# Low probabilities of two key tiles in the array's column halves, and a paced order of the attention's TensorE work

## The chip, the cores and the metric

The kernel runs on one core of one Trainium2 chip. The metric is the device time of one execution in microseconds. TensorE (PE) multiplies and transposes, ScalarE (ACT) and VectorE (DVE) work on tiles, GpSimd (POOL) and SyncE (SP) mostly issue DMAs here. Each engine takes its instructions in a fixed order.

## The reference

A decoder trunk of two layers, for one sequence of 2048 tokens and a model width of 1024, in float32: a Mamba-2 layer, then multi-head latent attention with 16 heads, a SiLU gate and an output projection, then a last RMS norm. The change is in the attention alone:

```python
def causal_block_attention(q_nope, q_rope, k_nope, k_rope, v):
    ...
        s = jnp.einsum('bqhd,bkhd->bhqk', q_nope[:, q0:kv_len], k_nope[:, :kv_len]) + \
            jnp.einsum('bqhr,bkr->bhqk', q_rope[:, q0:kv_len], k_rope[:, :kv_len])
        s = s.astype(jnp.float32) * scale
        mask = (q0 + local)[:, None] >= jnp.arange(kv_len)[None, :]
        p = jax.nn.softmax(jnp.where(mask, s, -jnp.inf), axis=-1).astype(v.dtype)
        outs.append(jnp.einsum('bhqk,bkhd->bqhd', p, v[:, :kv_len]))
```

A head has 96 score channels (64 + 32) and 64 value channels.

## The kernel before

The program runs the Mamba-2 layer, the projections of the second layer, then the attention (`heads`), then the output projection (`back`). Operands are kept as pairs: a value rounded to a shorter format (high) and what the rounding left (low), so that a few fast products give nearly float32.

**Jobs and rows.** The attention goes by jobs: one head and one block of 512 queries (`qb`, 0 to 3), 64 jobs in all. A job has four rows of 128 queries. A row's keys, up to the diagonal, are cut into score tiles of 256 to 512 keys: one tile a row in block 0, up to four in block 3. A score tile is three matmuls (high by high, high by low, low by high; lines L85, L86, L87 in `mm3`) into one PSUM bank tagged `mm`, of which there are four, and on a row's last tile a product that adds the mask (L903 or L905). VectorE takes each tile's maximum (L906) and, when the row is complete, the negated maximum of those (`nm`, L910). ScalarE then writes the exponentials of each tile (`Pr`, L918) with their sum. A bank is free for the score tile four later when its exponential is done. The exponentials of a row are emitted one by one ahead of the next tiles' score matmuls (`late`).

**Units.** A unit is one job and 128 keys (`kb`). `turn` transposes its probabilities with four TensorE transposes (fewer on the diagonal; L933) into a PSUM bank tagged `tr`, and `pair16` takes the bank to two float16 tiles: the high part on ScalarE (L116, "high copy"), the rest on VectorE (L117, "low copy", which reads the high one). `values` multiplies both with the values: the stationary operand `vals[h][:, kb, :]` holds 64 columns of high values and 64 of low values, so one matmul gives both halves of the output bank `O` (also `tr`, four banks in all). L943 is the product with the high probabilities, L944 the one with the low. `finish` takes the bank to memory (`Os`, L950), where a second DMA adds the lower 64 rows to the upper 64.

**What sets the order.** Inside the attention TensorE runs in the order in which the program is written (a manual schedule for this engine). ScalarE and VectorE are put in order by the scheduler of the tile framework. In TensorE's order, `ahead` emits the score tiles, and after each tile, from the 21st on (`LAG`), a table `CREDIT` says for this block, row and tile which work follows: T a turn, V the pair of value products of a unit turned at least two units ago (`DEPTH`). The work of a row stands mostly after its last tile.

Of the kernel before, what the change touches and what calls it, by code (L numbers as in the profile page):

```python
# [20 lines left out]
P = 128  # L21
# [17 lines left out]
EV0 = ['big', 'Xp', 'big', 'Sp', 'wsp']  # L39
EV1 = ['big', 'yT', 'Xp', 'big', 'Sp']  # L40
LAG = 20
DEPTH = 2
CREDIT = (
    (("VT",), ("TV",), ("VT",), ("TV",)),
    (("", "VTVT"), ("", "TTVV"), ("", "TTVV"), ("", "TTVV")),
    (("TT", "", "VVTV"), ("TV", "", "VTTV"), ("TV", "", "TTVV"), ("TTV", "", "TVV")),
    (("T", "", "", "VVTTVTV"), ("T", "V", "", "VTTVTV"), ("T", "V", "V", "TVTTV"), ("TV", "V", "", "TVTVT")),
)
MAGIC = 12582912.0
PSCALE = 32768.0  # L50
TINY = 2.0 ** -100
# [17 lines left out]
class Net:  # L69
# [793 lines left out]
    def heads(self, sp):  # L863
# [15 lines left out]
        def scores(h, qb, st):  # L879
# [8 lines left out]
            for j in range(4):  # L888
                qs = slice(j * P, (j + 1) * P)
                parts = cuts(qb * TB + (j + 1) * P)  # L890
                nb = len(parts)
                mx = self.t(sp, "mx", [P, 4], bufs=4)
                banks = []
                for n, (c0, w) in enumerate(parts):
                    if late:
                        late.pop(0)()
                    begun.append(0)
                    s = self.t(self.pp, "tr" if len(begun) <= 18 and len(begun) % 2 == 1 else "mm", [P, TB], bufs=4)
                    ks = slice(c0, c0 + w)
# [6 lines left out]
                    v.tensor_reduce(mx[:, n:n + 1], s[:, :w], AX.X, ALU.max)  # L906
                    banks.append((s, w))
                    yield CREDIT[qb][j][n]
                nm = self.t(sp, "nm", [P, 1], bufs=4)
                v.tensor_reduce(nm, mx[:, :nb], AX.X, ALU.max, negate=True)  # L910
                p = {}
                sm = self.t(sp, "sm", [P, 4], bufs=4)
                st["P"].append(p)

                def exp(n, j=j, nb=nb, parts=parts, banks=banks, nm=nm, p=p, sm=sm):
                    s, w = banks[n]
                    x = self.t(sp, "Pr", [P, TB], bufs=NP)
                    nc.scalar.activation(x[:, :w], s[:, :w], AF.Exp, bias=nm, accum_out=sm[:, n:n + 1])  # L918
# [9 lines left out]
        def turn(h, qb, kb, st):  # L928
# [3 lines left out]
            for j in range(jj, 4):  # L932
                nc.tensor.transpose(pt[:, j * P:(j + 1) * P], st["P"][j][kb], self.ident)  # L933
            c = slice(jj * P, TB)
            u = self.t(sp, "PTs", [P, 2, TB], F16, bufs=5)
            self.pair16(u[:, 0, c], u[:, 1, c], pt[:, c], PSCALE)
            return u[:, :, c], c

        def values(h, qb, kb, st, u, c):
            if kb == 0:  # L940
                st["O"] = self.t(self.pp, "tr", [P, TB], bufs=4)
            nk = 4 * qb + 4
            nc.tensor.matmul(st["O"][:, c], vals[h][:, kb, :], u[:, 0], start=kb == 0, stop=False)  # L943
            nc.tensor.matmul(st["O"][:, c], vals[h][:, kb, :], u[:, 1], start=False, stop=kb == nk - 1)  # L944
            if kb == nk - 1:
                finish(h, qb, st)

        def finish(h, qb, st):
# [19 lines left out]
        states = [{"P": []} for _ in jobs]  # L968
        sums = {}
        def ahead():  # L970
            for n, (h, qb) in enumerate(jobs):
                if qb == 0:
                    sums[h] = self.t(sp, "sum", [P, 16], bufs=3)
                yield from scores(h, qb, states[n])

        units = [(h, qb, kb, states[n]) for n, (h, qb) in enumerate(jobs) for kb in range(4 * qb + 4)]
        held = []

        def work(what):

            if what == "T" and units:
                a = units.pop(0)
                held.append((a, turn(*a)))
            elif what == "V" and held and (len(held) > DEPTH or not units):
                a, (u, c) = held.pop(0)
                values(*a, u, c)

        step = 0
        for credit in ahead():
            step += 1  # L990
            if step > LAG:
                for what in credit:
                    work(what)
        while units or held:
            work("T")
            work("V")


    def back(self):
# [190 lines left out]
```

## Time and profile before

| | us |
|---|---|
| median of three runs | 3243.08 |
| lowest, highest | 3242.1, 3247.14 |
| profiled execution | 3238.15 |
| its span | 3236.3 |
| attention, first score tile to last value product | about 2128 to 3050 of the span |
| TensorE busy | 3156.2 (98%) |
| VectorE busy | 2593.4 (80%) |
| ScalarE busy | 2055.2 (64%) |

The granted TensorE clock is 0.995 of full speed on average. A profile row names line, engine, operation, the tile written and the tiles read, and shapes; then come durations and, where an engine stood idle before, for how long and what ended that. A TensorE instruction's duration is longer than the time for which it holds the engine, since the next one starts into the array behind it; the distance from start to start, or from end to end, is the price of one.

### The profile page before, as it was taken

How to read it: one execution, taken by the hardware profiler on the slowest of the kernel's cores; microseconds unless marked ns; L12 is line 12 of the kernel's file. 1: busy time of each engine (PE TensorE's matmuls, PEld its weight loads, DVE VectorE, ACT ScalarE, POOL GpSimd, SP SyncE). 2: the span in 40 equal slices, each digit the busy share in tenths (PEclk: the TensorE clock that was granted, in tenths of full speed). 3: DMA queues.
4: the chain of work that ended last, by engine and by line, in shares of the span. 5: the costliest groups of instructions: out<-in, count | busy, mean ns of one | idle time of the engine just before them, and what ended most of it. 6: DMA issues, size and time to landing. Idle time of an engine off the chain costs nothing.

```text
span 3236.3 us, 50476 instructions
## 1 busy us (share of the span) xinstructions
PE 3156.2 (98%) x16708; PEld 2563.4 (79%) x16708; DVE 2593.4 (80%) x5490; ACT 2055.2 (64%) x5117; POOL 646.2 (20%) x842
## 2 busy tenths in 40 slices
PE   8999999999999999998999999999999999999998
PEld 6788888888888888887888888777777777777787
DVE  6988888889889888887776765668888888888675
ACT  5666666666657655666555554567777877778522
POOL 1221122221212222222211211222212212223100
PEclk9999999999999999999999999999999999999999
DMA  5333343333433334333466666753443434344385
GB/s 174 108 104 92 118 131 119 105 96 122 140 96 109 90 125 145 104 94 111 132 221 212 236 204 208 246 137 79 82 89 77 97 77 88 77 90 116 81 272 172
DMA packets 210572, 418.91 MB, mean 129 GB/s; under 512 B 27107, under 2 KB 68835, under 8 KB 208869
## 3 DMA queue, kind: packets, MB, share of 16 engines
q1 hardware_dynamic: 168900, 291.39, 28.9%
q0 software_dynamic: 41408, 124.29, 15.7%
q8 instruction: 132, 2.16, 0.3%
q14 instruction: 132, 1.07, 0.1%
HBM read 321.33 MB, written 94.24 MB: 128 GB/s over the span
## 4 chain that ended last, share of the span: by engine, by line
PE 44%; ACT 3%; DMA 2%; DVE 2%; issue 1%; SPq 0%; POOL 0%; ACTq 0%; DVEq 0%
PE mm L85 7%; PE mm L87 7%; PE mm L86 7%; PE tr L933 6%; PE tr L943 3%; PE tr L944 3%; PE tr L86 3%; PE tr L87 3%; PE tr L85 3%; ACT Pr L918 1%; DVE PTs L117 1%; ACT PTs L116 1%; DMA wraw<-in_kv_w_up_dram 1%; PE mm L905 1%; DMA wraw<-in_kv_w_down_dram 0%
## 5 line engine op out<-in xcount | busy, mean ns | idle before, releaser
L117 DVE SCALAR_TENSOR_TENSOR PTs<-tr,PTs 128x512 f16<-128x512 f32 (+3 forms) x640 | 374.7, 607 | 92.6 <-ACT PTs L116 86.0
L116 ACT ACTIVATE PTs<-tr 128x512 f16<-128x512 f32 (+3 forms) x640 | 328.2, 541 | 140.9 <-PE tr L933 140.0
L906 DVE TENSOR_REDUCE mx<-mm 128x1 f32<-128x512 f32 (+2 forms) x631 | 375.5, 607 | 45.4 <-PE mm L87 42.8
L918 ACT ACTIVATE Pr<-mm,nm 128x512 f32<-128x512 f32 (+2 forms) x631 | 395.1, 635 | 23.1 <-DVE nm L910 21.5
L108 ACT ACTIVATE wsp<-wraw 128x512 fp32r<-128x512 f32 (+1 forms) x452 | 251.1, 574 | 171.7 <-PE mm L87 82.4
L109 DVE TENSOR_TENSOR wsp<-wraw,wsp 128x512 fp32r<-128x512 f32 (+1 forms) x452 | 301.8, 680 | 69.7 <-ACT wsp L108 68.9
L85 PE MATMUL mm<-xT,wsp 128*128 128x512 f32 x800 | 321.0, 401 | 0.0
L933 PE MATMUL tr<-pack,Pr 128*128 128x128 f32 x2176 | 317.5, 273 | 0.9 <-ACT Os L950 0.8
L87 PE MATMUL mm<-xT,wsp 128*128 128x512 f32 x800 | 314.1, 393 | 0.0
L86 PE MATMUL mm<-xT,wsp 128*128 128x512 f32 x800 | 312.9, 391 | 0.0
L85 PE MATMUL mm<-K,xT 96*128 96x512 f32 (+2 forms) x639 | 286.7, 449 | 23.1 <-ACT Pr L918 21.7
L933 PEld LDWEIGHTS tr<-pack,Pr 128*128 128x128 f32 x2176 | 253.4, 141 | 49.3 <-ACT Os L950 1.6
L85 PE MATMUL mm<-wsp,xT 128*128 128x512 f32 (+1 forms) x640 | 242.1, 378 | 0.0
L86 PE MATMUL mm<-wsp,xT 128*128 128x512 f32 (+1 forms) x640 | 237.7, 371 | 0.0
L87 PE MATMUL mm<-wsp,xT 128*128 128x512 f32 (+1 forms) x640 | 237.5, 372 | 0.0
L87 PE MATMUL mm<-K,xT 96*128 96x512 f32 (+2 forms) x639 | 231.4, 362 | 0.0
L358 DVE SCALAR_TENSOR_TENSOR cacc<-craw,pack,cacc 128x512 f32<-128x512 f32 x288 | 216.5, 774 | 18.3 <-ACT cacc L356 17.8
L86 PE MATMUL mm<-K,xT 96*128 96x512 f32 (+2 forms) x639 | 231.1, 362 | 0.0
L496 POOL TENSOR_TENSOR Xp<-Xw,Xp 128x512 fp32r<-128x512 f32 x64 | 83.1, 1298 | 697.5 <-ACT Xp L495 393.1
L943 PE MATMUL tr<-PTs,xT 128*128 128x512 f16 (+3 forms) x640 | 222.0, 348 | 0.1
L538 ACT ACTIVATE Xw<-tr,d_wend 128x64 f32<-128x64 f32 x512 | 182.8, 358 | 58.7 <-DVE Xd L534 58.6
L944 PE MATMUL tr<-PTs,xT 128*128 128x512 f16 (+3 forms) x640 | 219.4, 347 | 0.0
(368 smaller groups left out, 8145.9 us busy)
## 6 DMA issues: line engine op xcount, KB each, us to landing
wraw<-in_ssm_w_in_dram SPq DMA_DIRECT2D x256, 256.0 KB, 2.8
big<-cumT SPq DMA_DIRECT2D x64, 512.0 KB, 4.0
wraw<-in_ssm_w_out_dram SPq DMA_DIRECT2D x128, 256.0 KB, 2.6
wraw<-in_ssm_w_in_dram SPq DMA_DIRECT2D x129, 128.0 KB, 2.2
xT<-qn_d POOLq DMA_DIRECT2D x64, 256.0 KB, 4.4
K<-kn_d POOLq DMA_DIRECT2D x15, 1024.0 KB, 9.2
wraw<-in_mla_w_uq_dram SPq DMA_DIRECT2D x36, 256.0 KB, 4.0
hx<-in_x_dram SPq DMA_DIRECT2D x16, 512.0 KB, 4.2
```

The source lines that it names most:

```text
L85: mm(out, l_hi, r_hi, start=start, stop=False)
L86: mm(out, l_hi, r_lo, start=False, stop=False)
L87: mm(out, l_lo, r_hi, start=False, stop=stop)
L108: nc.scalar.activation(hi, src, AF.Copy)
L109: nc.vector.tensor_tensor(lo, src, hi.bitcast(F32), ALU.subtract)
L116: self.nc.scalar.activation(hi, src, AF.Copy, scale=scale)
L117: self.nc.vector.scalar_tensor_tensor(lo, src, scale, hi, ALU.mult, ALU.subtract)
L906: v.tensor_reduce(mx[:, n:n + 1], s[:, :w], AX.X, ALU.max)
L918: nc.scalar.activation(x[:, :w], s[:, :w], AF.Exp, bias=nm, accum_out=sm[:, n:n + 1])
L933: nc.tensor.transpose(pt[:, j * P:(j + 1) * P], st["P"][j][kb], self.ident)
L943: nc.tensor.matmul(st["O"][:, c], vals[h][:, kb, :], u[:, 0], start=kb == 0, stop=False)
L944: nc.tensor.matmul(st["O"][:, c], vals[h][:, kb, :], u[:, 1], start=False, stop=kb == nk - 1)
```

## The change

`CREDIT` goes. Three things take its place.

`pair16` now writes the high and the low probabilities of a unit into two tiles (`PTh`, five buffers, and `PTl`, ten). `values` does the product with the high ones alone. The low ones are kept for four units and then multiplied by `lows`: four matmuls with the 64 columns of high values only. Units 0 and 2 of the four write the output bank's partitions 0 to 63, units 1 and 3 partitions 64 to 127, so that they use the left and the right half of the array's columns. The product of low probabilities with low values is no longer computed. `finish` is unchanged and adds both halves.

The work behind the score tiles is dealt out by time. Each score tile of `w` keys brings `S_US * w * rate * PACE` us of allowance, 15% of it at once and the rest when its row is complete; each turn, value product or group of low products spends its own price (`T_US`, `V_US`, `L_US`), and work goes on while the allowance is positive. A group of low products goes first, then a value product when more than two units are held, then a turn. A unit may be turned only when its job's last score tile is at least four score tiles back (`GAP`).

```diff
-CREDIT = (
-    (("VT",), ("TV",), ("VT",), ("TV",)),
...
+PACE = 1.04
+GAP = 4
+T_US, V_US, L_US, S_US = 0.436, 0.216, 0.45, 0.00137
@@
-                    yield CREDIT[qb][j][n]
+                    yield w, n == nb - 1
@@
-            u = self.t(sp, "PTs", [P, 2, TB], F16, bufs=5)
-            self.pair16(u[:, 0, c], u[:, 1, c], pt[:, c], PSCALE)
-            return u[:, :, c], c
+            hi, lo = self.t(sp, "PTh", [P, TB], F16, bufs=5), self.t(sp, "PTl", [P, TB], F16, bufs=10)
+            self.pair16(hi[:, c], lo[:, c], pt[:, c], PSCALE)
+            return (hi[:, c], lo[:, c]), c
@@
-            nc.tensor.matmul(st["O"][:, c], vals[h][:, kb, :], u[:, 0], start=kb == 0, stop=False)
-            nc.tensor.matmul(st["O"][:, c], vals[h][:, kb, :], u[:, 1], start=False, stop=kb == nk - 1)
-            if kb == nk - 1:
+            nc.tensor.matmul(st["O"][:, c], vals[h][:, kb, :], u[0], start=kb == 0, stop=False)
+            st["lo"].append((kb, u[1], c))
+
+        def lows(h, qb, st):
+            end = st["lo"][-1][0] == 4 * qb + 3
+            for i, (kb, l, c) in enumerate(st["lo"]):
+                d = slice(i % 2 * 64, i % 2 * 64 + 64)
+                nc.tensor.matmul(st["O"][d, c], vals[h][:, kb, 0:64], l, start=False, stop=end and i >= 2)
+            st["lo"] = []
+            if end:
                 finish(h, qb, st)
@@
+        def work(limit):
+            if owed:
+                h, qb, st = owed.pop()
+                lows(h, qb, st)
+                return L_US
+            ready = units and units[0][0] < limit
+            if held and (len(held) > DEPTH or not units):
+                (_, h, qb, kb, st), u = held.pop(0)
+                values(h, qb, kb, st, *u)
+                if kb % 4 == 3:
+                    owed.append((h, qb, st))
+                return V_US * part(qb, kb)
+            if ready:
                 a = units.pop(0)
-                held.append((a, turn(*a)))
...
+                held.append((a, turn(*a[1:])))
+                return T_US * part(*a[2:4])
+            return 0
...
+            limit = max([k + 1 for k in ended if k < n and ended[k] + GAP <= step], default=0)
+            if step <= LAG:
+                continue
+            share = PACE * rate * S_US * w
+            kept += share * (1 if last else 0.85)
+            if last:
+                allowed, kept = allowed + kept, 0.0
+            else:
+                allowed += share * 0.15
+            while allowed > 0:
+                t = work(limit)
+                if not t:
+                    allowed = min(allowed, 2.0)
+                    break
+                allowed -= t
```

The orders of the engines outside the attention are the same row by row; on each engine the number of instructions is the same. Lines of the new program differ by number: L931 is the old L933, L940 the product with the high probabilities, L949 a low product, L83 to L85 the score matmuls, L903 the mask, L916 the exponential, L904 and L908 the maxima, L114 and L115 the high and the low copy.

TensorE, at the border of two heads, before: the last unit rows ahead of the new head's first score tile (K_29297 are its keys), and the way to its second tile.

```order
L943 MATMUL tr_29732<-PTs_29769,xT_28498 128x512
L944 LDWEIGHTS xT_28498
L944 MATMUL tr_29732<-PTs_29769,xT_28498 128x512
...
L85 MATMUL mm_29845<-K_29297,xT_29038 128x256
...
L903 MATMUL mm_29845<-mk,idb 128x256
L943 LDWEIGHTS xT_28498
L943 MATMUL tr_29732<-PTs_29804,xT_28498 128x512
...
L933 MATMUL tr_29853<-pack,Pr_29432 128x128
...
L85 MATMUL mm_29867<-K_29297,xT_29038 128x256
```

The same place now (K_28831 are the new head's keys), with the start of each of the four tiles:

```order
L903 MATMUL mm_29372<-mk,idb 128x128
L931 MATMUL tr_29378<-pack,Pr_29056 128x128
...
L940 MATMUL tr_29231<-PTh_29326,xT_27992 128x512
L931 MATMUL tr_29386<-pack,Pr_29103 128x128
...
L940 MATMUL tr_29231<-PTh_29335,xT_27992 128x384
L83 MATMUL mm_29411<-K_28831,xT_28564 128x256
...
L83 MATMUL mm_29424<-K_28831,xT_28564 128x256
...
L83 MATMUL mm_29437<-K_28831,xT_28564 128x384
...
L83 MATMUL mm_29450<-K_28831,xT_28564 128x512
...
L931 MATMUL tr_29456<-pack,Pr_29183 128x128
```

Between the first two tiles of the head there was a value pair and a turn; now the first four tiles follow one another, and three transposes and two value products lie between the old head's last tile (mm_29372) and them.

VectorE, around the first row of the third block (three score tiles), before:

```order
L906 TENSOR_REDUCE mx_28504<-mm_28505 128x1
L922 TENSOR_REDUCE sum_28235<-sm_28489 128x1
L117 SCALAR_TENSOR_TENSOR PTs_28515<-tr_28510,PTs_28515 128x512
L117 SCALAR_TENSOR_TENSOR PTs_28523<-tr_28518,PTs_28523 128x512
L906 TENSOR_REDUCE mx_28504<-mm_28526 128x1
L906 TENSOR_REDUCE mx_28504<-mm_28531 128x1
L910 TENSOR_REDUCE nm_28551<-mx_28504 128x1
```

and now:

```order
L904 TENSOR_REDUCE mx_29682<-mm_29683 128x1
L904 TENSOR_REDUCE mx_29682<-mm_29688 128x1
L920 TENSOR_REDUCE sum_29405<-sm_29667 128x1
L115 SCALAR_TENSOR_TENSOR PTl_29699<-tr_29693,PTh_29698 128x512
L904 TENSOR_REDUCE mx_29682<-mm_29702 128x1
L115 SCALAR_TENSOR_TENSOR PTl_29715<-tr_29709,PTh_29714 128x512
L115 SCALAR_TENSOR_TENSOR PTl_29724<-tr_29719,PTh_29723 128x384
L908 TENSOR_REDUCE nm_29728<-mx_29682 128x1
```

The negated maximum stood right behind the row's last maximum; now two low copies of later units stand between them.

ScalarE, the four exponentials of the third row of the fourth block (L918, from nm_29753) and the high copies among them, before:

```order
L918 ACTIVATE Pr_29757,sm_29755<-mm_29680,nm_29753 128x512
L116 ACTIVATE PTs_29740<-tr_29735 128x512
L116 ACTIVATE PTs_29748<-tr_29743 128x512
L918 ACTIVATE Pr_29774,sm_29755<-mm_29695,nm_29753 128x512
L116 ACTIVATE PTs_29769<-tr_29764 128x512
L918 ACTIVATE Pr_29783,sm_29755<-mm_29704,nm_29753 128x512
L918 ACTIVATE Pr_29790,sm_29755<-mm_29718,nm_29753 128x384
```

and of the same row now (from nm_30181):

```order
L916 ACTIVATE Pr_30185,sm_30183<-mm_30110,nm_30181 128x512
L114 ACTIVATE PTh_30158<-tr_30153 128x512
L114 ACTIVATE PTh_30168<-tr_30163 128x512
L114 ACTIVATE PTh_30177<-tr_30173 128x384
L916 ACTIVATE Pr_30193,sm_30183<-mm_30117,nm_30181 128x512
L916 ACTIVATE Pr_30200,sm_30183<-mm_30125,nm_30181 128x512
L916 ACTIVATE Pr_30211,sm_30183<-mm_30133,nm_30181 128x384
```

Ahead of the exponential that frees the second bank stood two high copies; now three do, the last one of a unit turned just before the next row's first score tile.

More of the change, by code (lines that the diff above doesn't have):

```diff
@@ L967, in heads @@
         jobs = [(h, qb) for h in range(NH) for qb in range(NB)]
-        states = [{"P": []} for _ in jobs]
+        states = [{"P": [], "lo": []} for _ in jobs]
         sums = {}
@@ L973, in ahead @@
                     sums[h] = self.t(sp, "sum", [P, 16], bufs=3)
[L974 to L981, printed above, removed]
-                a = units.pop(0)
-                held.append((a, turn(*a)))
-            elif what == "V" and held and (len(held) > DEPTH or not units):
-                a, (u, c) = held.pop(0)
-                values(*a, u, c)
@@ L988, in heads, with part @@
-        step = 0
-        for credit in ahead():
-            step += 1
[L991 to L996, printed above, removed]
+                for w, last in scores(h, qb, states[n]):
+                    yield n, w, last
+        def part(qb, kb):
+            return (4 - max(kb - 4 * qb, 0)) / 4
+        units = [(n, h, qb, kb, states[n]) for n, (h, qb) in enumerate(jobs) for kb in range(4 * qb + 4)]
@@ new lines, in heads @@
+        held, owed = [], []
+        def work(limit):
[11 more added lines that the diff above has]
+            if ready:
+                a = units.pop(0)
+                held.append((a, turn(*a[1:])))
+                return T_US * part(*a[2:4])
+            return 0
@@ new lines, in heads @@
+        tiles = [(qb, kb) for qb in range(NB) for kb in range(4 * qb + 4)]
+        rate = sum((T_US + V_US) * part(*x) + L_US / 4 for x in tiles) / (S_US * P * sum(4 * (qb + 1) - 3 + j for qb in range(NB) for j in range(4)))
+        ended, step, allowed, kept = {}, 0, 0.0, 0.0
+        for n, w, last in ahead():
+            step += 1
+            ended[n] = step
+            limit = max([k + 1 for k in ended if k < n and ended[k] + GAP <= step], default=0)
[13 more added lines that the diff above has]
+                allowed -= t
@@ L999, in back @@
+        while work(len(jobs)):
+            pass
     def back(self):
```

5 lines of the change are left out of this document (removed).

## The prediction

> **What bounds the kernel now.** I read the page first, then the chain of waits in order of time, and then the timeline of one head of the attention. The page:
>
> ```profile
> span 3236.3 us, 50476 instructions
> PE 3156.2 (98%) x16708; PEld 2563.4 (79%) x16708; DVE 2593.4 (80%) x5490; ACT 2055.2 (64%) x5117; POOL 646.2 (20%) x842
> L944 PE MATMUL tr<-PTs,xT 128*128 128x512 f16 (+3 forms) x640 | 219.4, 347 | 0.0
> ```
>
> TensorE is busy 98% of the span. L944, the low value product, has 640 instructions, and only these are packed by the change. The chain shows how regular the attention is:
>
> ```profile
> 2494.37 1.29 DVE PTs L117 x2
> 2551.42 1.29 DVE PTs L117 x2
> ```
>
> The same pair of rows comes back after 57.05 us: that is one head, and there are 16. From the timeline (start, duration, engine), two rows in the fourth block of one head, and the stretch that comes back with this period:
>
> ```profile
> 2501.78 0.33 PE L944 MATMUL tr<-PTs,xT 128*128 128x384 f16 x1
> 2502.18 0.50 PE L85 MATMUL mm<-K,xT 96*128 96x512 f32 x1
> ...
> 2550.29 0.88 DVE L906 TENSOR_REDUCE mx<-mm 128x1 f32<-128x384 f32 x2
> 2550.79 1.08 ACT L116 ACTIVATE PTs<-tr 128x512 f16<-128x512 f32 x2
> 2551.40 0.60 PE L933 MATMUL tr<-pack,Pr 128*128 128x128 f32 x4
> 2551.42 1.29 DVE L117 SCALAR_TENSOR_TENSOR PTs<-tr,PTs 128x512 f16<-128x512 f32 x2 [0.26 <-ACT PTs L116]
> 2552.05 0.38 PE L944 MATMUL tr<-PTs,xT 128*128 128x512 f16 x1
> 2552.10 0.60 ACT L116 ACTIVATE PTs<-tr 128x512 f16<-128x512 f32 x1 [0.22 <-PE tr L933]
> 2552.63 0.15 DVE L910 TENSOR_REDUCE nm<-mx 128x1 f32<-128x4 f32 x1
> 2552.73 0.69 DVE L117 SCALAR_TENSOR_TENSOR PTs<-tr,PTs 128x512 f16<-128x512 f32 x1
> 2552.81 0.69 ACT L918 ACTIVATE Pr<-mm,nm 128x512 f32<-128x512 f32 x1
> 2553.39 0.19 ACT L918 ACTIVATION_READ_ACCUMULATOR Pr<-mm,nm 128x1 f32 x1
> 2553.49 0.68 ACT L918 ACTIVATE Pr<-mm,nm 128x512 f32<-128x512 f32 x1
> 2553.64 0.50 PE L85 MATMUL mm<-K,xT 96*128 96x512 f32 x1 [1.21 <-ACT Pr L918]
> ```
>
> Here TensorE does stand still. The four score banks are full, so a new row's first score (L85) waits for the old row's first exponential (L918), which waits for the row's maximum (L910), which stands in VectorE's queue behind two low copies (L117), which wait for ScalarE's high copies (L116). From the end of L944 (2552.43) to the end of L85 (2554.14) are 1.71 us. A 512 score takes 0.23, so 1.48 is stall. The first pair gives 2502.68 - 2502.11 = 0.57, so about 0.33. These two make 1.8 us of a head; the rest is TensorE's own work. So the attention is bound by TensorE, with the loop score, maximum, exponential, bank next behind it.
>
> **The unit prices**, from start to start in the TensorE timeline:
>
> ```profile
> 2511.55 0.39 PE L85 MATMUL mm<-K,xT 96*128 96x512 f32 x1
> 2511.77 0.39 PE L86 MATMUL mm<-K,xT 96*128 96x512 f32 x1
> 2512.00 0.39 PE L87 MATMUL mm<-K,xT 96*128 96x512 f32 x1
> 2522.77 1.04 PE L933 MATMUL tr<-pack,Pr 128*128 128x128 f32 x8
> 2523.65 0.38 PE L943 MATMUL tr<-PTs,xT 128*128 128x512 f16 x1
> 2523.87 0.38 PE L944 MATMUL tr<-PTs,xT 128*128 128x512 f16 x1
> 2524.08 0.38 PE L943 MATMUL tr<-PTs,xT 128*128 128x512 f16 x1
> ```
>
> A score tile of 512 is 3 x 0.23 = 0.70, a turn of four transposes 0.44 (8 in 0.88), a value product of 512 columns 0.216; narrower ones go with their columns. On the other engines, from the stretch above: a high copy holds ScalarE 0.48 (two in 1.08, one 0.60 long), a low copy holds VectorE 0.60, an exponential holds ScalarE 0.67 (2552.81 to 2553.49), and from its start to the score that gets its bank pass 0.83 (2552.81 to 2553.64). From a turn's last transpose leaving TensorE's queue to the high copy pass 0.26: its end trails by 0.16, and 2552.00 to 2552.10 is the rest.
>
> **Part one, the packing.** A head has 28 full value units and four each of 384, 256 and 128 columns. The groups of one head, with busy time, mean ns of one, idle time before:
>
> ```profile
> L943 PE MATMUL tr<-PTs,xT 128*128 128x512 f16 x28 | 10.6, 380 | 0.0
> L943 PE MATMUL tr<-PTs,xT 128*128 128x384 f16 x4 | 1.3, 326 | 0.0
> ...
> L906 DVE TENSOR_REDUCE mx<-mm 128x1 f32<-128x512 f32 x25 | 17.0, 685 | 2.7 <-PE mm L87 2.6
> L116 ACT ACTIVATE PTs<-tr 128x256 f16<-128x256 f32 x4 | 1.6, 401 | 2.3 <-PE tr L933 2.3
> L117 DVE SCALAR_TENSOR_TENSOR PTs<-tr,PTs 128x256 f16<-128x256 f32 x4 | 1.7, 420 | 0.6 <-ACT PTs L116 0.6
> L117 DVE SCALAR_TENSOR_TENSOR PTs<-tr,PTs 128x128 f16<-128x128 f32 x4 | 1.1, 283 | 0.3 <-ACT PTs L116 0.3
> ```
>
> Low products now: 28 x 0.216 + 4 x (0.16 + 0.11 + 0.055) = 7.36 us a head. After the change they come in ten groups of four, even tiles in columns 0 to 63, odd in 64 to 127. If two halves run at once, six full groups cost 2 x 0.216 and four diagonal groups 0.216 + 0.11: 2.59 + 1.30 = 3.9, a saving of 3.47 a head, **55 us** in all. If they run one after the other the saving is 0. No row of this trace shows two halves in flight, so these are the bounds. I take the full saving: the two products share neither array columns nor PSUM partitions. The Trainium skill (TensorE: Matmul & The Clock Gate, "Measured speedup vs the span model") gives 2.38 times for three column tiles; by that a pair saves somewhat less than half, an estimate of 45 to 50 us.
>
> **Part two, the order.** The count of instructions on ScalarE and VectorE is unchanged; their order and TensorE's is not. I read each row border in the new order, adding the prices along the queues from the row's last score to the score that needs its bank, and compare it with what TensorE has to do in between.
>
> *Start of a head.* The old order puts turns and values between the four short rows of the next head. The new one issues these four score tiles in one run, since the last job's units are held until four tiles after its end. They reuse the four banks of the row just ended. To the fourth tile TensorE has 2.0 us of work (three transposes, two values, three tiles). The chain needs: maximum 0.63 (the row's 0.685 less the 0.09 by which the next one overlaps, as with the low copies, and a hop), low copies of 256 and 128 columns 0.55 (0.42 and 0.28, less the same), L910 with its hop 0.18, three exponentials 2.0, the last to the score 0.83: 4.2. **Stall 2.2.** The first value of the new job then waits for a low copy to free its output bank: 0.4.
>
> *Third block, first row.* Two low copies (512 and 384) stand ahead of L910 again, and the row's last maximum behind a third. From its last score to the score that needs the bank 3.6 pass against 2.1 of work: **1.5**, the twin of the 1.48 above.
>
> *Fourth block.* After its first row a high copy stands ahead of the first exponential, and its turn ends only one unit before the score: 0.26 + 0.48 + 0.83 = 1.57 against 0.55, **1.0**. In the three later rows the same pattern (two or three high copies, then the exponential that frees the second bank) leaves 0.4, 0.2 and 0.2, and 0.7: **1.5**.
>
> *Diagonal units.* Three times a turn takes a bank 1.0 us after an earlier turn, while the way over a high and a low copy of 256 columns takes 0.26 + 0.40 + 0.42 and two hops, 1.2; twice 1.5 against 1.6 for 512. With some queueing **0.7**, the softest of the terms.
>
> Sum: 2.2 + 0.4 + 1.5 + 1.0 + 1.5 + 0.7 = 7.3 us a head, in place of 1.8. The same addition on the old order finds 1.4 and 0.2 where the trace has 1.48 and 0.33, so it errs low by a tenth to a fifth: 7.3 to 8.2. Net: 7.3 - 1.8 - 3.5 = +2.0, or +2.9 with the correction; I take +2.5, times 16 = **+40 us**. Bounds: no new stall, -55; all of it and no packing, +46 + 55 = +101. Queues elsewhere are not touched: work outside the attention keeps its order, and the output's two DMAs a job have tens of us to land.
>
> Against the profiled execution's 3238.15 (span 3236.3, 1.9 around it) that is 3278; the median of the runs shown is 4.9 above it. I predict **3280**.
>
> **The rivals.**
>
> *The waits melt.* VectorE and ScalarE have idle time, and a stall at one border gives both time to catch up for the next. If only the run at the head's start (2.2) and the first row of the third block (1.5) stay, the head changes by 3.7 - 1.8 - 3.5 = -1.6: -26, 3215 us. With all waits as today: 3187. For it: the sums treat borders singly, and the old order shows only two such stalls. Against it: each term above is a queue position, not a backlog. Faster, 0.24.
>
> *Even.* Stalls of 5.3 a head eat the saving exactly: 3243. 0.10.
>
> *The halves run in turn.* One mechanism: the second half's product starts only when the first leaves the array, as any two value products do now, 0.216 apart. The saving of 3.47 is gone: 3280 + 55, less what longer groups cover, about 3330. It decides from the first pair on. Against it: nothing but the disjoint outputs. 0.10.
>
> *Each change of array shape costs a drain.* A group enters and leaves the 64-column shape, 320 changes. If each let the array run empty, the tail of a product (0.38 long, next one 0.216 later) lies open, 0.16: +52, 3332. The trace has this shape once a block:
>
> ```profile
> 741.76 0.48 PE L86 MATMUL mm<-wsp,yT 128*128 128x512 f32 x1
> 742.08 0.63 PE L423 MATMUL tr<-xT,wdt 128*64 128x512 f32 x2
> ...
> 744.63 1.32 PE L423 MATMUL tr<-xT,wdt 128*64 128x512 f32 x5
> 745.79 0.40 PE L87 MATMUL mm<-wsp,yT 128*128 128x512 f32 x1
> 746.02 0.40 PE L85 MATMUL mm<-wsp,yT 128*128 128x512 f32 x1
> ```
>
> In: 742.24 to 742.71 for two products, 0.235 each. Out: 745.95 to 746.19, 0.24, then 0.23. No drain to see. 0.04. The Trainium skill (TensorEngine Tiling, "Key Properties") says that changing the tiling mode drains TensorE; by that rule this case would be the likely one, but the rows above disagree.
>
> **How the numbers follow.** My forecast has 0.52, with 3258 to 3305 as its own range. The two dear cases add 0.14, so slower has 0.66, same 0.10, faster 0.24; 0.2% (6.5 us) is about what a measurement here can tell from no change. The range, 3215 to 3325, leaves out about half of the faster cases and the dear end.
>
> **What would show it.** Right: L944's successor shows pairs that start well under 0.2 us apart; idle time before the first score matmul, ended by the exponential, grows from about 2 to 7 us a head, most of it in four short tiles in a row; a head takes 59 to 60 us; VectorE's share falls. Wrong: a head under 56 us, with that idle time at 2 to 3 us (then my queue sums fail), or pairs 0.2 us apart (then the packing fails).

## The result and the profile after

The changed kernel takes 3360.81 us (median of 3358.25 to 3361.7) against 3243.38 for the kernel before on the same chip: a ratio of 1.036, 95% interval 1.0347 to 1.0372. It is slower, as forecast, but by 117 us where 37 were predicted, and above the range. The profiled execution has a span of 3359.2 against 3236.3: 123 us to explain.

The page of the changed kernel, busy times and the costliest groups (busy, mean ns of one, idle time before and what ended it):

```profile
span 3359.2 us, 50328 instructions
PE 3227.3 (96%) x16708; PEld 2547.7 (76%) x16708; DVE 2600.9 (77%) x5490; ACT 2073.9 (62%) x5117; POOL 646.6 (19%) x842
...
L83 PE MATMUL mm<-K,xT 96*128 96x512 f32 (+2 forms) x639 | 294.7, 461 | 70.2 <-ACT Pr L916 68.1
```

VectorE and ScalarE do the same work as before in a longer time. TensorE's busy time has grown by 71 us although the packing was to take 55 away, and its idle time before the first score product of a tile is 70.2 us, 68.1 of it ended by the exponential; the same row of the kernel before reads:

```profile
L85 PE MATMUL mm<-K,xT 96*128 96x512 f32 (+2 forms) x639 | 286.7, 449 | 23.1 <-ACT Pr L918 21.7
```

Stretches of the changed kernel, three windows in a row and then two whole heads (length, busy time of each engine with its instructions, then granted clock, DMA share, GB/s):

```profile
2495.25:2498.66 3.41, 1.83 (x12) 1.25 (x12) 1.48 (x5) 2.27 (x7) 2.13 (x4) 1.00 0.59 128
2498.66:2502.08 3.42, 3.42 (x13) 2.40 (x13) 1.91 (x9) 2.58 (x10) 0.00 (x0) 0.50 0.99 203
2502.08:2505.49 3.41, 3.41 (x18) 2.45 (x17) 2.33 (x7) 1.83 (x5) 0.00 (x0) 0.50 0.46 91
...
2520.99:2583.57 62.58, 58.19 (x355) 40.24 (x354) 48.27 (x114) 45.94 (x126) 12.07 (x19) 1.00 0.38 77
2583.57:2650.47 66.90, 62.52 (x355) 43.70 (x354) 48.50 (x114) 46.60 (x126) 12.09 (x19) 0.92 0.36 72
```

Two costs show here. A head without any loss of clock takes 62.58 us against 57.05 before; the other one, with a mean clock of 0.92, takes 66.90. The first rows show what happens there: TensorE's clock falls to half for 6.83 us, right after a stretch in which it stood idle for 3.41 - 1.83 = 1.58 us. The attention has 17 such stretches at half clock, of 3.41 or 6.83 us; half of their length, 44 us, is the most they can cost. Nine of them (29 us) follow the wait at the start of a head, seven (12 us) the wait at the second row of a third block, and one (3 us) a wait for a value product. The kernel before has none in its attention.

The idle time stands at the borders that the prediction named. The head's start, all engines but the weight loads, with other rows left out:

```profile
2560.49 0.23 PE L903 MATMUL mm<-mk,idb 128*128 128x128 bf16 x1
...
2560.76 0.69 DVE L904 TENSOR_REDUCE mx<-mm 128x1 f32<-128x512 f32 x1 [0.76 <-PE mm L903]
...
2561.11 0.33 PE L940 MATMUL tr<-PTh,xT 128*128 128x384 f16 x1
2561.46 0.62 DVE L115 SCALAR_TENSOR_TENSOR PTl<-tr,PTh 128x256 f16<-128x256 f32 x2
2562.00 0.15 DVE L908 TENSOR_REDUCE nm<-mx 128x1 f32<-128x4 f32 x1
2562.18 0.69 ACT L916 ACTIVATE Pr<-mm,nm 128x512 f32<-128x512 f32 x1 [0.59 <-DVE nm L908]
2563.01 0.39 PE L83 MATMUL mm<-K,xT 96*128 96x256 f32 x1 [1.58 <-ACT Pr L916]
```

From the row's last product to the bank that its first exponential frees pass about 2.5 us: maximum, two low copies, negated maximum, exponential. TensorE has three transposes and two high products to do meanwhile, 0.7 us, and then stands.

And the packing. TensorE at one group in the changed kernel:

```profile
2515.79 0.38 PE L940 MATMUL tr<-PTh,xT 128*128 128x512 f16 x1
2516.10 0.14 PEld L949 LDWEIGHTS <-xT 128*64 128x64 f16 x4 [0.26 <-issue]
2516.10 0.62 PE L949 MATMUL tr<-PTl,xT 128*64 128x512 f16 x4
2516.65 0.33 PE L931 MATMUL tr<-pack,Pr 128*128 128x128 f32 x1
```

Four products in 0.62 us: within a pair the starts lie 3 ns apart, from pair to pair 0.24. The halves do run at once. But the first of them starts 0.31 after the product before it, where 0.216 is the distance between two value products, and the transpose behind the group starts 0.31 after the second pair. The group's first weight load (PEld) starts only then as well, 0.31 after the start of the product before it.

To compare all runs I took, over the whole attention, the distance of each TensorE instruction's end from the end before it, less the usual one for its kind. What is over 0.06 us, outside the half-clock stretches and the groups' edges, is "waits"; it holds more than the idle time in the rows above, for example 1.85 us where the row at the head's start shows 1.58. "Half clock" is half the length of those stretches, from the first score tile to the last value product. Groups of low products are measured from end to end too: at full clock, a full group takes 0.552 us where four full-width products take 0.864, and what follows it ends 0.15 (a transpose) to 0.20 (a score) later than usual; a diagonal group takes 0.443 in place of 0.544, with the same 0.15 to 0.20 behind it, and so loses 0.05 to 0.1.

| kernel | time | waits, us | half clock, us |
|---|---|---|---|
| before | 3241 to 3243 | 37 | 0 |
| after | 3360.8 | 125 | 44 |
| new order, no packing | 3342.5 | 120 | 17 |
| old order, packing | 3288.8 | 95 | 2 |
| old order, fours at full width | 3273.8 | 69 | 2 |
| after, 96 groups in the left half | 3364.5 | 117 | 19 |
| after, zero products at the head's start | 3338.2 | 102 | 15 |
| after, pace 0.99 | 3311.6 | 103 | 7 |
| after, maxima first | 3317.0 | 102 | 22 |
| after, pace 0.99 and maxima first | 3275.1 | 75 | 3 |
| old order, packing, maxima first | 3265.6 | 67 | 3 |
| before, maxima first | 3226.0 | 21 | 0 |
| before without low products | 3302.6 | 177 | 24 |
| the same, maxima first | 3206.2 | 115 | 0 |

### The profile page after: what moved, and what is told of

It is laid out like the page before. It is cut to its first block, busy times and chain, and to the rows that moved or that the text cites. A ratio compares the mean times of both kernels' runs of the same rounds, so it can differ in the third digit from the quotient of the medians.

```text
span 3359.2 us, 50328 instructions
## 1 busy us (share of the span) xinstructions
PE 3227.3 (96%) x16708; PEld 2547.7 (76%) x16708; DVE 2600.9 (77%) x5490; ACT 2073.9 (62%) x5117; POOL 646.6 (19%) x842
## 4 chain that ended last, share of the span: by engine, by line
PE 42%; ACT 5%; DVE 2%; DMA 2%; issue 2%; SPq 0%; POOL 0%; ACTq 0%; DVEq 0%
PE mm L83 8%; PE mm L85 6%; PE mm L84 6%; PE tr L931 6%; PE tr L84 3%; PE tr L85 3%; PE tr L83 3%; PE tr L949 2%; PE tr L940 2%; ACT Pr L916 2%; ACT PTh L114 2%; DVE PTl L115 1%; PE mm L903 1%; DMA wraw<-in_mla_w_in_dram 0%; DMA wr<-in_mla_w_out_dram 0%
## 5 line engine op out<-in xcount | busy, mean ns | idle before, releaser
L115 DVE SCALAR_TENSOR_TENSOR PTl<-tr,PTh 128x512 f16<-128x512 f32 (+3 forms) x640 | 374.1, 608 | 137.7 <-ACT PTh L114 131.4
L904 DVE TENSOR_REDUCE mx<-mm 128x1 f32<-128x512 f32 (+2 forms) x631 | 375.9, 609 | 117.6 <-PE mm L85 53.3
L114 ACT ACTIVATE PTh<-tr 128x512 f16<-128x512 f32 (+3 forms) x640 | 326.0, 536 | 224.2 <-PE tr L931 221.2
L916 ACT ACTIVATE Pr<-mm,nm 128x512 f32<-128x512 f32 (+2 forms) x631 | 391.7, 635 | 42.6 <-DVE nm L908 40.3
L931 PE MATMUL tr<-pack,Pr 128*128 128x128 f32 x2176 | 368.8, 287 | 1.5 <-ACT Pr L916 1.1
L83 PE MATMUL mm<-K,xT 96*128 96x512 f32 (+2 forms) x639 | 294.7, 461 | 70.2 <-ACT Pr L916 68.1
L931 PEld LDWEIGHTS tr<-pack,Pr 128*128 128x128 f32 x2176 | 269.2, 148 | 88.0 <-issue 24.9
L83 PE MATMUL mm<-xT,wsp 128*128 128x512 f32 x800 | 321.0, 401 | 0.0
L85 PE MATMUL mm<-xT,wsp 128*128 128x512 f32 x800 | 314.1, 393 | 0.0
L83 PE MATMUL mm<-wsp,xT 128*128 128x512 f32 (+1 forms) x640 | 241.9, 378 | 0.5 <-ACT craw L350 0.5
L85 PE MATMUL mm<-wsp,xT 128*128 128x512 f32 (+1 forms) x640 | 237.3, 372 | 0.0
L85 PE MATMUL mm<-K,xT 96*128 96x512 f32 (+2 forms) x639 | 237.1, 371 | 0.0
L84 PE MATMUL mm<-K,xT 96*128 96x512 f32 (+2 forms) x639 | 236.6, 370 | 0.0
L83 PEld LDWEIGHTS mm<-K,xT 96*128 96x128 f32 x639 | 123.8, 194 | 147.3 <-ACT Pr L916 122.0
L940 PE MATMUL tr<-PTh,xT 128*128 128x512 f16 (+3 forms) x640 | 226.8, 359 | 3.5 <-ACT PTh L114 2.8
```

Source lines behind the costliest of these rows:

```text
L83: mm(out, l_hi, r_hi, start=start, stop=False)
L84: mm(out, l_hi, r_lo, start=False, stop=False)
L85: mm(out, l_lo, r_hi, start=False, stop=stop)
L114: self.nc.scalar.activation(hi, src, AF.Copy, scale=scale)
L115: self.nc.vector.scalar_tensor_tensor(lo, src, scale, hi, ALU.mult, ALU.subtract)
L940: nc.tensor.matmul(st["O"][:, c], vals[h][:, kb, :], u[0], start=kb == 0, stop=False)
```

## The experiments

### What the order and the packing cost, each alone

The new order, the low products over all 128 columns, in the same fours:

```diff
-                d = slice(i % 2 * 64, i % 2 * 64 + 64)
-                nc.tensor.matmul(st["O"][d, c], vals[h][:, kb, 0:64], l, start=False, stop=end and i >= 2)
+                nc.tensor.matmul(st["O"][:, c], vals[h][:, kb, :], l, start=False, stop=end and i == 3)
```

> The new order with the packing undone: each low product goes over all 128 columns, values' low halves included, at the same places in the order. My theory of the result (3360.8): the row borders of the new order wait 5.8 us a head longer (+93), the change into and out of the half-column shape costs 0.32 us a group (ten a head, +51), which eats the 55 the packing saves, and the TensorE clock falls to half for some us after the run of four tiles at each head's start (+37). By it this kernel is about as slow as the changed one: 3350 to 3380. The rival, that packing earns its 55 and the order alone loses 172, says 3410 to 3420.

Measured: 3342.45, ratio 1.0311 (1.0295 to 1.0326). That is 8 us under the theory's range and far from the rival's. The order without packing costs 101 us, 83 of it in waits; the low products' place in fours is part of this order. The packing does not earn 55 on top of it: the packed kernel is the slower one, by 18. Of half clock it has 27 us more; but for that it would be at most some 9 ahead.

The old order (`CREDIT`), with the packing: after every fourth value product a group of four low products. The two tiles of probabilities and `lows` are those of the changed kernel and are left out here.

```diff
...
+            if kb % 4 == 3:
+                lows(h, qb, st)
...
```

> The old order (the table of turns and value products) with the packing: the value product of every fourth unit is followed by the group of four low products in column halves. My theory: 55 saved, 51 lost to the shape changes, so 3232 to 3250, near the kernel before. The rival that packing earns 55: about 3190.

Measured: 3288.82, ratio 1.0142 (1.0125 to 1.0159). A miss for both: the packing alone makes the kernel slower by 47 us. Its row:

```profile
L85 PE MATMUL mm<-K,xT 96*128 96x512 f32 (+2 forms) x639 | 286.0, 448 | 48.3 <-ACT Pr L918 44.3
```

The groups themselves are not the reason. Within the 160 groups 36.4 us are saved against full width, behind them 27.7 are lost: the packing earns 8.7 us of 55. The waits grow from 37 to 95.

To part the groups' place from the packing, the same with full-width products in the fours (the line as in the first diff):

> The old order with the low products in fours after each fourth value unit, as in the run that packs alone (3288.8), but each over all 128 columns: no halves, no change of shape. It parts the 47 us of that run into the place of the low products and the packing. Theory (packing gives 36.4 us in the groups and loses 27.7 at their ends, and the rest is cover that went from the borders without a group): the fours alone cost most of it, 3275 to 3300. Rival (shape changes and halves cost the 47): 3241 to 3255.

Measured: 3273.75, ratio 1.0102 (1.0087 to 1.0117), 1 us below the expected range. Keeping the low products back for a group of four, in tiles of their own, costs 32 us in waits, with no half in use; what of this the separate tiles do by themselves was not run. The packing, on top of that, adds another 15: it takes 9 us out of the groups, and 26 come back as waits.

What the shape costs without the gain: 96 of the 160 groups of the changed kernel with all four products in the left half, one after the other.

```diff
-                d = slice(i % 2 * 64, i % 2 * 64 + 64)
+                d = slice(i % 2 * 64, i % 2 * 64 + 64) if end else slice(0, 64)
```

> The changed kernel, but in the 96 full groups (all but a job's last) all four low products go to the left column half, so they run one after the other: still the 64-column shape, never two halves. Two theories of the 0.32 us: (a) it is the shape: the gaps at these groups stay, and each is 0.43 longer: +41, about 3402; (b) it is that two halves are loaded and run together: the gaps at these groups go and each is 0.43 - 0.32 = 0.11 longer: +11, about 3372.

Measured: 3364.54, ratio 1.0381 (1.0364 to 1.0399). It is below both expectations, and by its time alone this run would mislead. The groups did get longer, 0.981 by ends in place of 0.552, 41 us over 96 of them, and the clock came back by 25 us and the waits by 8. A group of the fours at full width, then one in the left half:

```profile
2511.76 0.38 PE L942 MATMUL tr<-PTh,xT 128*128 128x512 f16 x1
2511.76 0.75 PEld L950 LDWEIGHTS <-xT 128*128 128x128 f16 x4
2511.98 1.03 PE L950 MATMUL tr<-PTl,xT 128*128 128x512 f16 x4
2512.84 0.38 PE L933 MATMUL tr<-pack,Pr 128*128 128x128 f32 x2
```

```profile
2520.68 0.38 PE L940 MATMUL tr<-PTh,xT 128*128 128x512 f16 x1
2520.99 1.05 PE L949 MATMUL tr<-PTl,xT 128*64 128x512 f16 x4
2521.97 0.33 PE L931 MATMUL tr<-pack,Pr 128*128 128x128 f32 x1
```

From the high product to the transpose 1.08 us at full width, 1.29 in the left half, 0.86 in two halves. The columns stream for as long in the first two, so 0.21 is what going into the 64-column shape and out of it costs from start to start; from end to end it is 0.117 on the way in and 0.15 to 0.20 on the way out, 46 us for 160 groups (18.7 and 27.7). The product that does not change shape pays nothing: 0.216 in, no delay out. The weight loads show one difference: at full width the first load of the group starts together with the product before it (2511.76), at a change of shape 0.31 after that start. The Trainium skill (TensorEngine Tiling (Array Packing), "Key Properties") says that a change of the tiling mode drains TensorE; these rows agree with it and give the price, but that it is the array that drains they do not show.

### The half clock

Nine zero products at each head's start (seven before the first score tile, one before each of the next two), where TensorE waits anyway (`zero` is a tile of zeros, `opened` lists the output banks; their lines are left out):

```diff
...
+                    if qb == 0 and h:
+                        for _ in range((7, 1, 1, 0)[j]):
+                            nc.tensor.matmul(opened[-1], zero, vals[h - 1][:, 0:4, :].rearrange("p k d -> p (k d)"),
+                                             start=False, stop=False)
...
```

> The changed kernel with nine products by a stationary operand of zeros (512 columns, 0.216 us each), added to the output bank that is open, in the run of four score tiles at each head's start: seven ahead of the first tile, one ahead of the second and the third, where TensorE waits 1.9, 0.2 and 0.3 us. They add work only where it waits. If the half clock is set off by that idle time and costs about 37 us: the stretches of half clock go and the time is 3320 to 3330. If the half clock falls where TensorE waits anyway and costs nothing: 3355 to 3370.

Measured: 3338.21, ratio 1.03 (1.0284 to 1.0315). 29 us of added work, and the kernel is 22.6 us faster than without. The waits fall from 125 to 102, so 23 of the 29 us fit into them and 6 are added time. Nine stretches at half clock of 3.41 us are left, all behind the second row of a third block, whose wait of 1.6 us is unchanged; 44 us of loss became 15. The result lies between the two expectations: 29 us less of half clock and 6 of added work are the 23 gained, so by this run the half clock costs what half of its length says.

The other way to fill the head's start is to have units ready:

```diff
-PACE = 1.04
+PACE = 0.99
```

> The changed kernel with one number altered: the pace at which turning and value work is allotted, 1.04 of what comes in, becomes 0.99, so that the store of ready units does not run dry. In the trace of the changed kernel the first score tile of a head begins 0.71 us of TensorE work after the last tile of the head before it, and waits 1.85 us; with the clock at half for 6.83 or 3.41 us behind it. Counted from the written order with the durations of the trace (0.436 a turned unit, 0.216 a high product, 0.70 a group), that cover becomes 2.5 to 3.2 us. Theory (the waits are missing cover, and the half clock follows the idle time at the head start): the waits at the first three tiles of a head, 2.3 us, go, which is 37 us; the cover at the third block's second row grows from 2.1 to 2.7, another 0.5 a head or 8 us; the fourth block loses some 0.5 a head or 8 us; the half clock falls from 17 stretches, 44 us lost, to 3 or fewer: 3360.8 - 37 - 8 + 8 - 35 = 3289, between 3280 and 3310. Rival one (as much work as comes in is spread, so a border that gains cover takes it from another, and the waits stay 7.5 to 8 us a head): only the clock comes back, 3325 to 3335. Rival two (neither the order's pace nor the head start matters): 3355 to 3365.

Measured: 3311.55, ratio 1.0217 (1.0203 to 1.0231); 49 us gained, 2 short of the theory's range. Four stretches of half clock are left, 37 us of loss gone; with 22 us fewer waits that makes 59, of which 49 reached the time, so half of the length is an upper bound here. The head's start went as expected: the first three tiles wait 0.3 us in place of 2.2. But the waits in all fell only from 125 to 103. At the score tiles of the other blocks, outside stretches at half clock, they grew from 5.0 to 5.6 us a head: in the third block from 1.9 to 2.3 (its second row less, the other rows more), in the fourth they stayed at 3.1. Rival one is right in part: the pace deals out the same work, and some of what one border gets another lacks. By the program's own count of allowance, at 1.04 it runs out of ready units once in each head, and always at the border to the next one; that wait was also long enough to halve the clock.

### The chain over VectorE

Four kernels with the same edit (the last one with pace 0.99 besides): the maximum of a tile and the negated maximum of a row get priority over low copies in VectorE's order.

```diff
+                    with self.tc.high_priority(100):
+                        v.tensor_reduce(mx[:, n:n + 1], s[:, :w], AX.X, ALU.max)
-                    v.tensor_reduce(mx[:, n:n + 1], s[:, :w], AX.X, ALU.max)
...
+                with self.tc.high_priority(100):
+                    v.tensor_reduce(nm, mx[:, :nb], AX.X, ALU.max, negate=True)
-                v.tensor_reduce(nm, mx[:, :nb], AX.X, ALU.max, negate=True)
```

> The changed kernel with the order of VectorE alone altered: the maximum of a score tile and the row's negated maximum are put ahead of low copies that do not yet hold anyone up. In the changed kernel's trace two low copies (1.16 us) stand between the last maximum of the third block's first row and its negated maximum, and 0.62 us of copies before the one at the head start; in one head 11 copies stand so, which become 7. Theory (the chain from a row's last tile over VectorE and ScalarE to the free bank ends the waits, and copies lengthen it): each of the five large waits (1.65, 1.85, 0.86, 0.50, 0.75 us) shortens by 0.3 to 0.7, together 1.2 to 2.2 us a head, 19 to 35 us, and some of the half clock goes with the head start: 3315 to 3342. Rival (the waits are TensorE's missing work alone, and ScalarE's queue ends them): 3352 to 3365.

Measured: 3316.95, ratio 1.0235 (1.0221 to 1.0249). The theory's low end. On the mean of the heads the wait at the third block's second row falls from 1.64 to 0.65 and that of the first tile of the fourth block's second row from 0.86 to 0.04 (its second tile then waits 0.84 in place of 0.38), and half the loss of clock is gone.

> The kernel before, with the same edit of VectorE's order and nothing else. Its waits at score tiles are 1.42 us (fourth block, second row), 0.34 (third row) and some 0.3 of small ones, 2.1 a head. Theory (the chain over VectorE ends them): 0.7 to 1.4 us a head go, 11 to 22 us: 3219 to 3231, ratio 0.993 to 0.997. Rival (low copies put later hold the value products up, or ScalarE ends the waits): 3238 to 3250.

Measured: 3225.99, ratio 0.995 (0.9937 to 0.9964): half a per cent faster than the kernel before, and inside the theory's range. Its row:

```profile
L85 PE MATMUL mm<-K,xT 96*128 96x512 f32 (+2 forms) x639 | 288.3, 451 | 5.6 <-ACT Pr L920 4.2
```

The wait at the fourth block's second row, 1.43 on the mean of the heads, is 0.43; 16 us of waits are gone, and the 15 us of time with them.

> The old order with the packed low products (as in the run that packs alone, 3288.8), and VectorE's order altered as above. The waits at score tiles of that run are some 5.6 us a head against 2.1 before, at nine places, while the packing itself gives 36.4 us within the groups and loses 27.7 behind them. Theory (packing shortens the TensorE work that covers the chain of a row, so a shorter chain gives it back): 1.0 to 2.0 us a head go, 16 to 32 us: 3257 to 3273, more than the kernel before gains by the same edit. Rival (the waits come from the groups' places, not from the chain's length): 3280 to 3292.

Measured: 3265.57, ratio 1.0076 (1.0062 to 1.0089): 23 us gained, against 15 for the kernel before, as the theory had it. With packing the chain's length counts for more.

> The changed kernel with both edits that helped it: pace 0.99 (3311.6, -49) and maxima first (3317.0, -44). If they act on different waits: 3361 - 93 = 3268. Theory: both take from the same half clock (38 and 24 of 44 us), so that part is counted once, and the waits that pace 0.99 leaves, 7.1 a head, shrink by the 1.7 a head that the maxima gave before: 3361 - 49 - 27 = 3285, between 3275 and 3295. If the pace leaves nothing for it: 3305 to 3315.

Measured: 3275.1, ratio 1.0108 (1.0093 to 1.0123). Nearer to the sum of both gains (3268) than to 3285, though inside the theory's range: the waits fall to 75, more than I had counted, most of it at the score tiles of the third block, from 2.3 us a head with the pace alone to 1.0.

### What TensorE's work at a border is worth

The kernel before without its second value product, so that the low probabilities do not enter the result. It is the limit of any packing: 7.36 us of TensorE work a head less, 118 us in all.

```diff
-            nc.tensor.matmul(st["O"][:, c], vals[h][:, kb, :], u[:, 0], start=kb == 0, stop=False)
-            nc.tensor.matmul(st["O"][:, c], vals[h][:, kb, :], u[:, 1], start=False, stop=kb == nk - 1)
+            nc.tensor.matmul(st["O"][:, c], vals[h][:, kb, :], u[:, 0], start=kb == 0, stop=kb == nk - 1)
```

> The kernel before, without its second value product (low probabilities times values), so the result lacks that term; the low copies are still made. It takes 7.36 us of TensorE work from each head, 118 us in all, twice what packing could ever take. If TensorE's work sets the time: 3241 - 118 = 3123. Theory (between a row's last score and the score that needs its bank TensorE's work is only cover for the chain over VectorE and ScalarE, so what is taken there comes back as a wait): the borders lose 0.43 to 0.86 us each. The four of the fourth block wait already or are within 0.1 us of it, so all 2.4 us taken there come back; of the third block's 2.4 or so, half to all, as the packed run waits 0.2 to 1.0 there; of the shorter rows' 2.5 little. 4 to 5.5 of 7.36 come back: 3241 - 16 x (1.9 to 3.4) = 3187 to 3211; not faster at all, 3230 to 3270, if VectorE's order turns for the worse with it as in the packed run.

Measured: 3302.61, ratio 1.0187 (1.0171 to 1.0202). With 118 us of work taken away the kernel is 61 us slower. No time that I had named goes so far. The waits grow from 37 to 177 and bring 24 us of half clock. Two parts of it can be read at the fourth block's second row (from the row's last score to the score that needs its bank):

```profile
2583.95 0.23 PE L905 MATMUL mm<-mk,idb 128*128 128x128 bf16 x1
...
2584.88 0.41 DVE L906 TENSOR_REDUCE mx<-mm 128x1 f32<-128x256 f32 x1
...
2585.51 1.89 DVE L117 SCALAR_TENSOR_TENSOR PTs<-tr,PTs 128x512 f16<-128x512 f32 x3 [0.22 <-ACT PTs L116]
2585.71 0.38 PE L943 MATMUL tr<-PTs,xT 128*128 128x512 f16 x1
2587.32 0.15 DVE L910 TENSOR_REDUCE nm<-mx 128x1 f32<-128x4 f32 x1
2587.50 0.69 ACT L918 ACTIVATE Pr<-mm,nm 128x512 f32<-128x512 f32 x1 [0.93 <-DVE nm L910]
...
2588.33 0.50 PE L85 MATMUL mm<-K,xT 96*128 96x512 f32 x1 [2.24 <-ACT Pr L918]
```

TensorE has 2.0 us of work in place of 2.6, that is the cover. And the negated maximum stands behind three low copies, 1.89 us: in the order that the framework's scheduler writes for VectorE, 20 low copies of one head stand between a row's last maximum and its negated maximum, against 8 before. So the chain is longer as well. With the maxima first, that part goes:

> As the run without low products (that term is left out of the result), with the maxima ahead of the low copies on VectorE; the kernel before with that edit alone is 3226. If TensorE's work sets the time: 3226 - 118 = 3108. Theory (a row's chain sets it): the shorter chain gives more here than the 15 us it gave the kernel before, since there are more waits: 30 to 90 us under the run without low products, and 3180 to 3215 in all, so that of 118 us taken from TensorE at most 45 reach the time.

Measured: 3206.16, ratio 0.9891 (0.9875 to 0.9908): inside the expected range, 96 us under the run before. The same place of this run:

```profile
2537.45 0.23 PE L905 MATMUL mm<-mk,idb 128*128 128x128 bf16 x1
...
2538.13 0.68 DVE L117 SCALAR_TENSOR_TENSOR PTs<-tr,PTs 128x512 f16<-128x512 f32 x1
...
2538.73 0.15 DVE L912 TENSOR_REDUCE nm<-mx 128x1 f32<-128x4 f32 x1
...
2540.18 0.50 PE L85 MATMUL mm<-K,xT 96*128 96x512 f32 x1 [0.45 <-ACT Pr L920]
```

From the last product to the score 2.73 us in place of 4.38. The waits, 115 us, are still three times those of the kernel before: of 118 us taken from TensorE, 20 reach the time (3226 to 3206). The rest comes back as waits, 94 us more than in the kernel before with the maxima first. Not all of that need be the chain's own length: 13 low copies of a head still stand between last and negated maxima, against 6 there. With 20 us for all of the low products' work, a packing that takes away less than half of it could hardly have earned its 55 us in this schedule, whatever the change of shape had cost; that is inferred, since no run here changes the shape for nothing.

## Why the prediction was wrong

Forecast: +40 us on the profiled execution, from waits of 7.3 to 8.2 a head in place of 1.8, less 55 us of packing. Point by point:

- **The pairs run at once: right.** 3 ns between their starts, 0.24 to the next pair.
- **The packing saves 55 us: wrong, the first of two steps that failed.** It saves 8.7. The change of array shape went into the sum at nothing. As a rival ("each change of array shape costs a drain") it was priced at 52 us and given 0.04, because the L423 rows show no gap. It costs 0.27 to 0.31 us a group, 46 us in all; I had argued it away from another kind of product. Those rows hold an f32 product with the same 64 columns, and the weight load of the first of them starts 0.17 after the start of the product before; why there is no gap there, no run here tells. The 64 diagonal groups, short in columns, even lose.
- **The waits: right.** Taken over the attention they are 125 us, 7.8 a head, against 7.3 to 8.2. By place, in the head without loss of clock: head's start 1.85 (2.2 said) and 0.5 in its next tiles, third block 1.64 (1.5), fourth block 0.9 (1.0) and 1.9 (1.5), diagonal units and other small ones about 1.1 (1.1). The base was 2.3 and not 1.8, so the net is 5.5 where I took 6.0, 8 us less in all.
- **The clock: not in the sum at all, the second step that failed.** The predicted 2.2 us of idle time at each head's start and the 1.5 of the third block each stood in one piece, and I asked only what they cost, not what they do to TensorE's clock. Up to 44 us, 29 behind the first and 12 behind the second; two runs that filled the head's start lost 29 and 37 us of it and were 23 and 49 us faster.
- **The sum.** 40 - 8 + 46 (packing) + 44 (clock, at most) = 122, and the spans differ by 123. That the time went up, as forecast, rests on the waits, and that step was right; the size was missed by the other two.
- **The signs named beforehand.** A head of 59 to 60 us: 62.6 without a drop of the clock, 64.9 on average. Idle time before the first score product, ended by the exponential, up; VectorE's share from 80 to 77%: both came. The upper bound of the costs, +101, was no bound, since the clock was not in it, and the range ended below even that.
- **"The waits melt", given 0.24:** they did not; most borders waited about as long as the sum for each alone said.

A miss of the runs themselves: I costed the packing alone at no new waits (3232 to 3250), that is, I took the low products for work that sets the time. They were cover.

## What to carry to other kernels

Before taking work from an engine that is 98% busy, ask at each border whether that work sets the time or covers a chain on other engines; here 118 us less of it made the kernel slower until the chain was shortened. A shorter chain (an edit that puts the maxima first) gained 15 us on the kernel before, where the packing lost 47. A wait that returns in every cycle is to be priced with what it does to the clock, and a change of array shape by a row of the same kind of product.

## What the hardware showed that was not expected

- Two 64-column float16 products into different halves start 3 ns apart, but going into that shape costs 0.117 us and leaving it 0.15 to 0.20, whether two halves are used or one; the weight load at such a change starts 0.31 after the start of the product before, where it starts together with it without a change.
- TensorE's clock falls to half in stretches of 3.41 or 6.83 us whose starts, counted modulo 3.4133, agree within 0.01 us in one execution, over all 17 of them. In the changed kernel's attention the 3.41 us ahead of such a stretch held 1.04 to 1.58 us of idle time, never one whole idle window; some windows with as much brought no drop, and in the kernel before 1.21 us, once a head, never did. The idle time alone does not decide it: in the run of the new order without packing a drop came after 0.92 us, and none after a window with 1.95. The Trainium skill (TensorE: Matmul & The Clock Gate, Part 1) gives a free-running window of 3413 ns, with which the trace agrees, and an idle window as the condition for half clock; here a window idle for under half its length was enough.
